# Low parts, decayed queries and masks in pieces of at most 512 columns, and a tie rule for activations, in a hybrid decoder step

## The chip, the cores and the metric

The kernel runs on one core of a Trainium2 chip. The metric is the device time of one execution in microseconds (us); the time given for a kernel is the median of several runs. Beside the runs there is one profiled execution, from which the trace comes. Its span runs from the first to the last instruction.

The engines are named as in the profile: PE is TensorE (matmuls; PEld its weight loads), DVE is VectorE, ACT is ScalarE, POOL is GpSimd, SP is SyncE, which issues most DMAs.

## The reference

One layer of a decoder for 1024 prompt tokens and 8 samples of 8 tokens each, 1088 columns in all, with a model width of 1024. Two branches work on the same input: sparse attention, in which a small indexer scores all keys and 256 are kept for each query, and gated linear attention (GLA). Both are projected, merged by gates, normalised, and followed by an MLP of width 4096. Cut to what matters here:

```python
def indexer_scores(q_idx, w_idx, k_idx):
    dots = jnp.einsum('bqhd,bsd->bqhs', q_idx, k_idx).astype(jnp.float32) * (IDX_DIM ** -0.5)
    w = w_idx.astype(jnp.float32) * (IDX_HEADS ** -0.5)
    return jnp.einsum('bqhs,bqh->bqs', jax.nn.relu(dots), w)
...
    def step(s, inp):
        qx, kx, vx, ax = inp
        cum = jnp.cumsum(ax, axis=-2)
...
        q_t = qx * jnp.exp(cum)
        k_t = kx * jnp.exp(-cum)
        att = jnp.where(causal, jnp.einsum('bhcd,bhed->bhce', q_t, k_t), 0.0)
        o = jnp.einsum('bhce,bhev->bhcv', att, vx) + jnp.einsum('bhcd,bhdv->bhcv', q_t, s)
...
def residual_block(x, mix_out, ln1_g, ln1_b, w_ff1, w_ff2, ln2_g, ln2_b):
    h = layer_norm(DN_ALPHA * x + mix_out, ln1_g, ln1_b)
    ff = jnp.square(jax.nn.relu(h @ w_ff1)) @ w_ff2
    return layer_norm(DN_ALPHA * h + ff, ln2_g, ln2_b)
```

The samples attend to 4096 cached keys each, which are read from a paged cache by a page table, for the indexer (64 wide) and for the attention (2 heads of 64).

## The kernel before

**Two parts of every number.** Matmuls of full precision are made of three faster ones. Each fp32 operand is split in a high part, which is a copy in the type fp32r, and a low part, which is the operand less its high part. A product is then high x high + high x low + low x high; the helper `mm3` issues the three. The high part is made by ScalarE (`act.activation(..., AF.Copy)`), the low part by a subtraction on VectorE or GpSimd, which the helper `sub` decides. Names in the profile follow this: `xh`, `xl`; `wh`, `wl`; `kih` and `kir` (the index keys' high part, and the raw page, which its low part overwrites); `ckh` and `ckl` (cached keys); `a` (both parts of an activation in one tile).

**An order chosen at build time.** The program is written by many generators (streams), for instance `idx_sample`, `gla_pre`, `at_scores` and `main`. Each yields what it needs next. The class `Order` asks every stream when its needs would be met and lets the first that is ready issue its next piece; the times come from `Clock`, which holds a modelled time for each engine and adds a modelled cost for every instruction. `Clock` also models that VectorE and GpSimd hold each other up on most of their operations. The engine queues then run in the order written, each waiting for the data of its instructions. `sub` reads the same modelled times: it takes GpSimd where that engine's time, plus 0.0021 us for each column, comes out before VectorE's, plus 0.00104 for each. So an edit of one instruction moves what is written after it, also on other engines and in streams that it doesn't touch. All instructions go through the helper at L266, so every row of the profile has that line, and work is told apart by the names of its tiles. The tokens stand in columns, in three chunks of 384, 384 and 320 (`CH`).

**The places that the change touches.**

- `idx_sample` (L880): the index keys of the samples come in 16 pages of 128x1024. `split(n)` copies page n to `kih` on ScalarE and subtracts into `kir`. Then `chunk` issues three matmuls `pss` for each 512 columns of the page: `kih`, `kir`, `kih`.
- `masks` (L1106): the masks of the prompt's query tiles, `msk`, are scaled by BIG on GpSimd, one instruction for each query tile, up to 1024 columns wide.
- `gla_pre` (L1291), once for each of four heads: the queries `gq` are multiplied by the decay `ge` on GpSimd, all 1088 columns, then the keys `gk` by its inverse `cu` on VectorE. `gla` (L1331) starts with `psas`, which needs the sample's 64 columns (the last) of both, and pads the sample's queries into `gqz`, 128x512, on GpSimd.
- `k_split` (L2404): the cached keys of the samples come in 32 pages of 128x1024 (two halves of 512 columns, one for each of two samples); ScalarE makes `ckh`, `sub` makes `ckl`, and `psc` matmuls use both. Their scores are summed into `as`, and VectorE adds the mask `msk` and takes the maximum in one custom instruction.
- `ff1_out` (L2670): after the eight matmul triples of a hidden block (`pf1`, in the profile `pf<-h,w`) ScalarE makes `fr`, the positive part, VectorE multiplies it by the matmul's result again to square it, ScalarE copies the high part into `a`, and `sub` makes the low part. The MLP works in groups: for the chunks 0 and 1, eight groups of four hidden blocks, in which the last activation is `a31` (block 3, chunk 1). The second matmuls (`pf2`, in the profile `pf<-a,w`) of a group follow its `pf1`, and meet `a31` as the last of the group's activations.

The stretches, in time: projections, indexer and GLA to about 885 us of the profile; output projections and the start of the MLP to 1155; the MLP of chunks 0 and 1 with the samples' attention beside it to about 1700; the samples' own output projections and the MLP of chunk 2 to the end.

Of the kernel before, what the change touches and what calls it, by code (L numbers as in the profile page):

```python
# [18 lines left out]
OP = mybir.AluOpType  # L19
# [4 lines left out]
P = 128  # L24
TP = 1024
TS = 64
T = TP + TS
# [8 lines left out]
CH = ((0, 384), (384, 384), (768, 320))  # L36
BIG = float(2.0 ** 100)
# [19 lines left out]
IAHEAD = 3  # L57
IFROM = 7
LATE_I = 1.5
FREER = 0.3  # L60
VAHEAD = 1
SCRATCH = 4096
# [30 lines left out]
def f32(ap):  # L93
    return ap.bitcast(F32)
# [292 lines left out]
def front(ph, tc, env, A, O):  # L387
    nc = tc.nc
    clock = env["clock"]
    pe, dve, act, pool, sp = env["eng"]  # L390
# [52 lines left out]
    def sub(out, a, b, late=0.0):  # L443

        n = out.free_size() if callable(out.free_size) else out.free_size
        if clock.t["pool"] + 0.0021 * n < clock.t["dve"] + 0.00104 * n + late:
            pool.tensor_tensor(out, a, b, op=OP.subtract)
        else:
            dve.tensor_sub(out, a, b)
# [179 lines left out]
    for c, (c0, n) in enumerate(CH):  # L629
        for k in range(KT):  # L630
            if c == 0 and k in (0, 4):
                h, l, r = (x[:, k:k + 4] for x in wtop)
                act.activation(h, r, AF.Copy)
                dve.tensor_sub(l, r, f32(h))
            s = slice(c0, c0 + n)
            r = xr[k - k % 2, c][:, k % 2, :n]
            act.activation(xh[k][:, s], r, AF.Copy)
            dve.tensor_sub(xl[k][:, s], r, f32(xh[k][:, s]))
        if c == 0:
            h, l, r = wnext  # L640
# [43 lines left out]
    bcol = csg("bcol", [P, 8, 64], BF)  # L684
# [146 lines left out]
    qz = page("qz", F32R, [P, 4, 2, P])  # L831
# [48 lines left out]
    def idx_sample():  # L880
        dve.memset(ss[1][0:64, TP:T], NEG)

        def split(n):
            r = raw[n]
            h = page(f"kih{n}", F32R, [P, 1024])
            act.activation(h, f32(r), AF.Copy)
            sub(r, f32(r), f32(h), LATE_I)
            raw[n] = (h, r)
        yield lambda: s_wtok.done
        cq = iota_f("cq", [4, 8, 8], [[0, 4], [0, 8], [1, 8]])  # L890
# [8 lines left out]
                                 selw, op0=OP.mult, op1=OP.mult)  # L899
# [206 lines left out]
    def masks(g, qts, gte):  # L1106
        if not mk:
            yield room("pg", 4)
        for i, grp in enumerate(MKP if not mk else ()):
            msk = page(f"msk{i}", BF, [P, 2 * T])  # L1110
            o = 0
            for qt in grp:
                mk[qt] = msk[:, o:o + (qt + 1) * P]
                o += (qt + 1) * P
        for j, qt in enumerate(qts):
            yield from fin(scp[qt], g.u[:, j:j + 1].bitcast(F32), mk[qt], gte)
            pool.tensor_scalar(mk[qt], mk[qt], BIG, None, op0=OP.mult)

    def top_first():
        yield lambda: s_ip.done  # L1120
# [170 lines left out]
    def gla_pre(h):  # L1291
# [32 lines left out]
        yield [cu]  # L1324
        act.activation(e, cu, AF.Exp, scale=1.0 / 16)
        act.activation(cu, cu, AF.Exp, scale=-1.0 / 16)
        pool.tensor_tensor(g["q"], g["q"], e, op=OP.mult)
        yield [cu]
        dve.tensor_tensor(g["k"], g["k"], cu, op=OP.mult)

    def gla(h):  # L1331
# [17 lines left out]
        dve.tensor_sub(vl[:TS], vs[:TS], f32(vh[:TS]))  # L1349
        pool.memset(f32(vl[TS:]), 0.0)  # L1350
        qz = small("gqz", 512).rearrange("p (a b) -> p a b", b=TS)
        pool.tensor_tensor(qz, q[:, None, TP:T].to_broadcast([P, 8, TS]), bcol, op=OP.mult)
        st = {}

        def half(i):
# [684 lines left out]
def back(ph, tc, env, A, O):  # L2040
# [20 lines left out]
    def own(name, shape, dt=F32, bufs=1):  # L2061
        return clock.take(pgs.tile(shape, dt, name=name, tag=name, bufs=bufs), name, "own " + name, bufs)

    def sub(out, a, b):
        n = out.free_size() if callable(out.free_size) else out.free_size
        if clock.t["pool"] + 0.0021 * n < clock.t["dve"] + 0.00104 * n:
            pool.tensor_tensor(out, a, b, op=OP.subtract)
        else:
            dve.tensor_sub(out, a, b)
# [334 lines left out]
    def k_split(n):  # L2404
        r = kraw.pop(n)
        h = wide(f"ckh{n}")
        l = wide(f"ckl{n}")
        act.activation(h, r, AF.Copy)
        sub(*(x.rearrange("p a b -> p (a b)") for x in (l, r, f32(h))))
        return h, l  # L2410

    def v_load(n):
# [257 lines left out]
    def ff1_out(ps, f, c, a):  # L2670
        n = CH[c][1]
        r = small("fr")
        act.activation(r[:, :n], ps[:, :n], AF.Relu)
        dve.tensor_tensor(r[:, :n], r[:, :n], ps[:, :n], op=OP.mult)
        t = page(f"a{f}{c}")
        act.activation(t[:, 0, :n], r[:, :n], AF.Copy)
        sub(t[:, 1, :n], r[:, :n], f32(t[:, 0, :n]))
        a[f, c] = (t[:, 0, :n], t[:, 1, :n])

    def ff2_pair(ws, c, a, np_):  # L2680
# [196 lines left out]
```

## Time and profile before

| | before |
|---|---|
| median of 3 runs | 2000.62 us (2000.35 to 2002.07) |
| the profiled execution | 2002.63 us |
| its span | 2000.9 us, 34496 instructions |
| mean granted TensorE clock | 0.997 |
| index pages' low parts, 128x1024 | 8 on VectorE (median 1227 ns), 8 on GpSimd (2402 ns) |
| cache pages' low parts, 128x1024 | 22 on VectorE (mean 1328 ns), 10 on GpSimd (2452 ns) |
| activations' low parts, 128x384 | 28 on VectorE (mean 587 ns), 36 on GpSimd (1018 ns) |

How rows of the profile are read: in the timeline, a row is start, length, engine, line, operation, tiles written <- tiles read, shapes and the count of like instructions in a row; in square brackets stands the engine's idle time before it and what ended that. In the groups by form, behind the bar stand the busy time in all, the mean of one in ns, and idle time before them. A row of waits is engine, tile <- what it waited for, then us in all, times, and the longest. A busy share near 100% on PE says only that matmuls were under way, since a matmul's recorded length overlaps the next one's.

### The profile page before, as it was taken

What the parts mean: (1) busy time and instruction counts of PE and PEld (TensorE: products, weight loads), DVE (VectorE), ACT (ScalarE), POOL (GpSimd) and SP (SyncE); (2) the same over time, 40 slices, a digit from 0 to 9 for tenths busy, and PEclk for the clock granted to TensorE, in tenths of its full rate; (3) what the DMA queues carried; (4) which work ended last, traced back from release to release, by engine and by line L of the source; (5) the groups of instructions that cost most, each with busy time, mean ns of one, the idle gap of its engine ahead of it and who ended that gap; (6) DMA issues with size and microseconds to landing.
All of it is one profiled execution on the core that took longest, in us unless ns stands there. A gap on an engine that the chain in (4) does not pass through costs nothing.

```text
span 2000.9 us, 34496 instructions
## 1 busy us (share of the span) xinstructions
PE 1977.4 (99%) x12341; PEld 1914.6 (96%) x12341; DVE 1288.1 (64%) x2704; ACT 1132.7 (57%) x2235; POOL 781.1 (39%) x640
## 2 busy tenths in 40 slices
PE   9999999999999999999999999999999999999998
PEld 8888999999999999999999999999999999999997
DVE  8887988777646856651366567777674445676635
ACT  6688778798667376660125345555654333455543
POOL 5133232232411422132233335646565543454455
PEclk9999999999999999999999999999999999999998
DMA  9564302213132243274751245545452354145542
GB/s 323 197 199 145 129 22 75 91 33 121 33 129 80 74 135 101 76 225 148 253 198 53 61 122 147 156 149 173 123 165 83 92 168 138 49 152 165 183 148 90
DMA packets 185164, 260.31 MB, mean 130 GB/s; under 512 B 22160, under 2 KB 121488, under 8 KB 184992
## 3 DMA queue, kind: packets, MB, share of 16 engines
q1 hardware_dynamic: 177440, 232.67, 36.6%
q0 software_dynamic: 7552, 25.43, 4.2%
q8 instruction: 97, 1.59, 0.3%
q14 instruction: 75, 0.61, 0.1%
HBM read 208.52 MB, written 49.51 MB: 129 GB/s over the span
## 4 chain that ended last, share of the span: by engine, by line
PE 64%; DVE 3%; ACT 2%; issue 2%; POOL 1%; DMA 1%; SPq 0%; ACTq 0%; POOLq 0%; DVEq 0%
PE pf L266 32%; PE gate L266 8%; PE pwo L266 5%; PE pmb L266 5%; PE gb L266 2%; PE pma L266 2%; PE psq L266 2%; PE pov L266 2%; PE ppt L266 2%; PE pob L266 1%; PE psc L266 1%; DVE as L266 1%; PE pst L266 1%; POOL w L266 0%; SPq L266 0%
## 5 line engine op out<-in xcount | busy, mean ns | idle before, releaser
L266 PE MATMUL pf<-a,w 128*128 128x384 f32 (+1 forms) x2304 | 398.6, 329 | 3.3 <-POOL a L266 1.3
L266 PE MATMUL pf<-h,w 128*128 128x384 f32 (+1 forms) x2304 | 395.2, 329 | 0.0
L266 PEld LDWEIGHTS pf<-a,w 128*128 128x128 f32 x2304 | 379.4, 188 | 7.8 <-ACT a L266 2.2
L266 PEld LDWEIGHTS pf<-h,w 128*128 128x128 f32 x2304 | 380.3, 188 | 2.9
L266 POOL TENSOR_TENSOR wl<-wr,wh 128x512 fp32r<-128x512 f32 (+1 forms) x135 | 171.4, 1291 | 405.1 <-ACT wh L266 319.3
L266 POOL TENSOR_TENSOR w<-wr,w 128x512 fp32r<-128x512 f32 x135 | 191.9, 1430 | 127.4 <-ACT w L266 118.4
L266 ACT ACTIVATE w<-wr 128x512 fp32r<-128x512 f32 x256 | 147.7, 619 | 34.1 <-PE pf L266 18.2
L266 DVE TENSOR_TENSOR w<-wr,w 128x512 fp32r<-128x512 f32 x121 | 124.4, 1033 | 51.8 <-ACT w L266 50.4
L266 DVE TENSOR_TENSOR acc<-acc,pf 128x384 f32<-128x384 f32 (+1 forms) x152 | 81.3, 538 | 82.1 <-PE pf L266 81.5
L266 PE MATMUL gate<-xh,wh 128*128 128x384 f32 (+1 forms) x384 | 130.1, 339 | 0.0
L266 PE MATMUL gate<-xh,wl 128*128 128x384 f32 (+1 forms) x384 | 125.6, 327 | 0.0
L266 PE MATMUL gate<-xl,wh 128*128 128x384 f32 (+1 forms) x384 | 125.6, 327 | 0.0
L266 POOL TENSOR_TENSOR a<-fr,a 128x384 fp32r<-128x384 f32 (+1 forms) x52 | 50.7, 976 | 181.4 <-ACT a L266 175.6
L266 ACT ACTIVATE wh<-wr 128x1024 fp32r<-128x1024 f32 (+1 forms) x76 | 75.2, 995 | 78.7 <-PE pmb L266 55.4
L266 ACT ACTIVATE a<-fr 128x384 fp32r<-128x384 f32 (+1 forms) x96 | 48.7, 507 | 105.8 <-DVE fr L266 105.8
L266 DVE TENSOR_TENSOR fr<-fr,pf 128x384 f32<-128x384 f32 (+1 forms) x96 | 50.7, 529 | 74.8 <-ACT fr L266 74.0
L266 ACT ACTIVATE jkb<-sc,gb_f 128x896 int8<-128x896 f32 (+2 forms) x96 | 86.1, 897 | 15.5 <-DVE gb_f L266 14.2
L266 ACT ACTIVATE fr<-pf 128x384 f32<-128x384 f32 (+1 forms) x96 | 44.6, 465 | 81.0 <-PE pf L266 79.9
L266 DVE TENSOR_SCALAR_CACHE_REDUCE jk<-sc,ga_f 128x1024 int8<-128x1024 f32 (+2 forms) x96 | 88.4, 921 | 2.2
L266 DVE CUSTOM_DVE_ANT_0 pp<-psq,msk 128x512 f32<-128x512 f32 (+3 forms) x96 | 51.2, 553 | 52.0 <-PE psq L266 45.4
L266 PE MATMUL psv<-wh,xh 128*128 128x256 f32 x288 | 80.8, 285 | 0.0
L266 PE MATMUL psv<-wl,xh 128*128 128x256 f32 x288 | 80.3, 283 | 0.0
(532 smaller groups left out, 5123.5 us busy)
## 6 DMA issues: line engine op xcount, KB each, us to landing
wr<-wff SPq DMA_DIRECT2D x254, 256.0 KB
wr<-w SPq DMA_DIRECT2D x42, 512.0 KB
ckr<-kT SPq DMA_DIRECT2D x256, 64.0 KB
ga_s<-gate SPq DMA_DIRECT2D x16, 544.0 KB
ci_s<-cig SPq DMA_DIRECT2D x16, 512.0 KB
kir<-ci_s SPq DMA_DIRECT2D x16, 512.0 KB
mgp<-ga_s SPq DMA_DIRECT2D x16, 384.0 KB
qa_s<-qa SPq DMA_DIRECT2D x8, 544.0 KB
```

Of the source, the lines that this page charges most:

```text
L266: r = f(*a, **k)
```

## The change

Five edits, in one diff:

- the index pages' low parts are made in two subtractions of 512 columns, each of which chooses its engine for itself;
- the scaling of the masks is cut at every 512 columns;
- the decay of the queries is cut in three, along the chunks 384, 384 and 320, and the padding of the sample's queries in two of 256;
- the cache pages' low parts are made in two subtractions of 512 columns, each choosing its engine;
- the activations' low parts go to GpSimd only if it comes out at least 0.5 us ahead by the modelled times (`A_LOW`); before, any lead was enough.

```diff
+A_LOW = 0.5
...
             act.activation(h, f32(r), AF.Copy)
-            sub(r, f32(r), f32(h), LATE_I)
+            for s in (slice(0, 512), slice(512, 1024)):
+                sub(r[:, s], f32(r[:, s]), f32(h[:, s]), LATE_I)
...
-            pool.tensor_scalar(mk[qt], mk[qt], BIG, None, op0=OP.mult)
+            for k0 in range(0, (qt + 1) * P, 512):
+                m = mk[qt][:, k0:min(k0 + 512, (qt + 1) * P)]
+                pool.tensor_scalar(m, m, BIG, None, op0=OP.mult)
...
-        pool.tensor_tensor(g["q"], g["q"], e, op=OP.mult)
+        for c0, n in CH:
+            s = slice(c0, c0 + n)
+            pool.tensor_tensor(g["q"][:, s], g["q"][:, s], e[:, s], op=OP.mult)
...
-        pool.tensor_tensor(qz, q[:, None, TP:T].to_broadcast([P, 8, TS]), bcol, op=OP.mult)
+        for s in (slice(0, 4), slice(4, 8)):
+            pool.tensor_tensor(qz[:, s], q[:, None, TP:T].to_broadcast([P, 4, TS]), bcol[:, s], op=OP.mult)
...
-    def sub(out, a, b):
+    def sub(out, a, b, sooner=0.0):
...
-        if clock.t["pool"] + 0.0021 * n < clock.t["dve"] + 0.00104 * n:
+        if clock.t["pool"] + 0.0021 * n + sooner < clock.t["dve"] + 0.00104 * n:
...
-        sub(*(x.rearrange("p a b -> p (a b)") for x in (l, r, f32(h))))
+        for i in range(2):
+            m = l.shape[1] // 2
+            sub(*(x[:, i * m:(i + 1) * m].rearrange("p a b -> p (a b)") for x in (l, r, f32(h))))
...
-        sub(t[:, 1, :n], r[:, :n], f32(t[:, 0, :n]))
+        sub(t[:, 1, :n], r[:, :n], f32(t[:, 0, :n]), A_LOW)
```

The edits move instructions on every engine from 119 us of the profile on. The three places below are the ones that the prediction speaks of. The added line shifts the helper from L266 to L267, and the numbers in the names count tiles, so a tile's number differs between the kernels.

The first is TensorE where the first index page is used, around 119 to 122 us (`ka` and `va` are matmuls of the projections, `pss` those of the index scores). Before:

```order
L266 MATMUL ka_2_1526<-xh7_125,wl5_0_1067 128x320
L266 MATMUL pss_1570<-kih0_1512,qz_314 128x512
L266 MATMUL pss_1570<-kir00_1506,qz_314 128x512
L266 MATMUL pss_1570<-kih0_1512,qz_314 128x512
L266 MATMUL pss_1576<-kih0_1512,qz_314 128x512
L266 MATMUL pss_1576<-kir00_1506,qz_314 128x512
L266 MATMUL pss_1576<-kih0_1512,qz_314 128x512
L266 MATMUL va_0_1610<-xh0_118,wh6_0_1290 128x384
```

And after, from the eighth of twelve `va` matmuls that now stand behind the same `ka`:

```order
L267 MATMUL va_0_1595<-xl2_128,wh6_0_1290 128x384
L267 MATMUL va_0_1595<-xh2_120,wl6_0_1291 128x384
L267 MATMUL va_0_1595<-xh3_121,wh6_0_1290 128x384
L267 MATMUL va_0_1595<-xl3_129,wh6_0_1290 128x384
L267 MATMUL va_0_1595<-xh3_121,wl6_0_1291 128x384
L267 MATMUL pss_1608<-kih0_1512,qz_314 128x512
L267 MATMUL pss_1608<-kir00_1506,qz_314 128x512
L267 MATMUL pss_1608<-kih0_1512,qz_314 128x512
L267 MATMUL pss_1614<-kih0_1512,qz_314 128x512
L267 MATMUL pss_1614<-kir00_1506,qz_314 128x512
L267 MATMUL pss_1614<-kih0_1512,qz_314 128x512
L267 MATMUL va_0_1595<-xh4_122,wh6_0_1290 128x384
```

So the six `pss` have moved behind twelve `va`. On GpSimd at the same place, before (`sc` are the prompt's index scores, whose diagonal is masked, `wl` the low part of a weight):

```order
L266 AFFINE_SELECT sc7_557<-sc7_557 128x128
L266 TENSOR_TENSOR kir01_1508<-kir01_1508,kih1_1567 128x1024
L266 TENSOR_TENSOR wl7_0_1607<-wr7_0_1288,wh7_0_1606 128x512 x2
L266 TENSOR_TENSOR kir10_1582<-kir10_1582,kih4_1676 128x1024
L266 TENSOR_TENSOR kir11_1641<-kir11_1641,kih5_1764 128x1024
```

and after:

```order
L267 AFFINE_SELECT sc7_557<-sc7_557 128x128
L267 TENSOR_TENSOR kir00_1506<-kir00_1506,kih0_1512 128x512
L267 TENSOR_TENSOR kir01_1508<-kir01_1508,kih1_1568 128x512 x2
L267 TENSOR_TENSOR kir02_1510<-kir02_1510,kih2_1622 128x512
L267 TENSOR_TENSOR wl7_0_1592<-wr7_0_1288,wh7_0_1591 128x512 x2
```

One half of the first page, `kir00`, is on GpSimd now, behind the select; it was whole on VectorE.

The second place is GpSimd at the third group of four hidden blocks, around 1268 to 1281 us (`cv` are cached values, `w` MLP weights, `a30` and `a31` the group's last two activations). Before:

```order
L266 TENSOR_TENSOR cv31_14303<-cvr3_14171,cv31_14303 128x512
L266 DMA cvr4_14306<-vv,ix_v_302 128x512 x2
L266 TENSOR_TENSOR ckl12_14360<-ckr12_14084,ckh12_14359 128x1024
L266 TENSOR_TENSOR w29_0_14399<-wr29_0_13982,w29_0_14399 128x512
L266 TENSOR_TENSOR cv41_14442<-cvr4_14306,cv41_14442 128x512
```

and after:

```order
L267 TENSOR_TENSOR cv31_14302<-cvr3_14149,cv31_14302 128x512
L267 DMA cvr4_14305<-vv,ix_v_302 128x512 x2
L267 TENSOR_TENSOR ckl12_14371<-ckr12_14081,ckh12_14370 128x512
L267 TENSOR_TENSOR a30_14408<-fr_14405,a30_14408 128x384
L267 TENSOR_TENSOR ckl13_14450<-ckr13_14181,ckh13_14449 128x512
L267 TENSOR_TENSOR a31_14484<-fr_14481,a31_14484 128x384
L267 TENSOR_TENSOR cv41_14500<-cvr4_14305,cv41_14500 128x512
```

Page 12 has one half on GpSimd, and the group's last two activations, which were on VectorE, stand on GpSimd, with a half of page 13 between them.

The third place is ScalarE at the eighth group, around 1721 to 1727 us (`h` and `z` belong to the LayerNorm of chunk 2, `lr` is its root, `lq` are squares for its sum). Before:

```order
L266 ACTIVATE lr_19356<-plv_19352,eps_101 128x3
L266 ACTIVATE fr_19370<-pf1_19339 128x384
L266 ACTIVATE a30_19373<-fr_19370 128x384
L266 ACTIVATE h02_19395<-z02_18789,lnp_100 128x320
L266 ACTIVATE h12_19398<-z02_18789,lnp_100 128x320
L266 ACTIVATE h22_19402<-z22_18791,lnp_100 128x320
L266 ACTIVATE h32_19412<-z22_18791,lnp_100 128x320
L266 ACTIVATE h42_19422<-z42_18931,lnp_100 128x320
L266 ACTIVATE fr_19424<-pf1_19376 128x384
L266 ACTIVATE a31_19427<-fr_19424 128x384
```

and after:

```order
L267 ACTIVATE fr_19414<-pf1_19389 128x384
L267 ACTIVATE a30_19417<-fr_19414 128x384
L267 ACTIVATE lq_19435<-z42_19079 128x320
L267 ACTIVATE lq_19439<-z62_19155 128x320
L267 ACTIVATE lq_19449<-z62_19155 128x320
L267 ACTIVATE fr_19458<-pf1_19420 128x384
L267 ACTIVATE a31_19461<-fr_19458 128x384
L267 ACTIVATE w89_0_19464<-wr89_0_18944 128x512
L267 ACTIVATE w90_0_19500<-wr90_0_19169 128x512
L267 ACT_TABLE_LOAD
L267 ACTIVATE lr_19516<-plv_19512,eps_101 128x3
L267 ACTIVATE h02_19545<-z02_18914,lnp_100 128x320
```

Five LayerNorm rows stood between `a30` and the last activation's `fr`; three squares stand there now, and the LayerNorm comes after `a31`.

## The prediction

> **What bounds the kernel.** I read the busy times first, then the chain that ended last.
>
> ```profile
> PE 1977.4 (99%) x12341; PEld 1914.6 (96%) x12341; DVE 1288.1 (64%) x2704; ACT 1132.7 (57%) x2235; POOL 781.1 (39%) x640
> PE 64%; DVE 3%; ACT 2%; issue 2%; POOL 1%; DMA 1%; SPq 0%; ACTq 0%; POOLq 0%; DVEq 0%
> ```
>
> TensorE (PE) is busy for 1977.4 of 2000.9 us, and the change neither adds nor removes a matmul. VectorE (DVE) and GpSimd (POOL) have hundreds of microseconds free, so an instruction there costs only when PE waits for its result. The question is which PE waits go and which arise.
>
> The written-out PE order is the same in both kernels up to 119 us of the profile, from 885 to 1155, and from about 1880 to the end. I take those stretches over at their old time. The two stretches where it moves, and three short ones that I need below:
>
> ```profile
> 70.40:72.20 1.80, 0.21 (x2) 0.00 (x0) 1.71 (x6) 0.69 (x3) 0.00 (x0) 1.00 0.85 344
> 72.30:75.60 3.30, 3.18 (x9) 3.03 (x10) 3.30 (x7) 1.96 (x4) 0.00 (x0) 0.50 0.97 313
> 75.70:79.10 3.40, 3.40 (x24) 3.34 (x23) 3.34 (x6) 1.46 (x3) 0.00 (x0) 1.00 0.14 57
> 119.00:885.00 766.00, 761.36 (x5004) 724.04 (x5004) 542.68 (x1430) 566.48 (x1169) 214.82 (x172) 1.00 0.33 102
> 1155.00:1880.00 725.00, 721.67 (x4381) 707.24 (x4380) 460.08 (x769) 356.47 (x662) 369.55 (x289) 1.00 0.45 137
> ```
>
> The columns are the window, its length, the busy time and count of PE, PEld, DVE, ACT and POOL, the granted clock, the DMA share and GB/s. PE is idle for 766.00 - 761.36 = 4.6 us and 725.00 - 721.67 = 3.3 us: 8 us in all are within reach. A row counts idle only from a matmul's modelled end, 0.33 us after its start, while matmuls of 128x384 start every 0.176 us (21 take 3.87 us below: 3.54 / 20). So a wait loses about 0.15 us more than its row says: some 10 us for the dozen or so waits. What they wait for, in the first stretch and then in the second:
>
> ```profile
> PE ppr L266 <- ACT jka L266: 1.9, 4, 0.6
> PE pss L266 <- DVE kir L266: 1.4, 1, 1.4
> ...
> PE psas L266 <- DVE gk L266: 0.3, 1, 0.3
> ```
> ```profile
> PE pf L266 <- ACT a L266: 0.7, 1, 0.7
> ...
> PE pf L266 <- POOL a L266: 0.6, 1, 0.6
> ```
>
> The change touches four of these: key pages `kir`, decayed keys `gk` (behind the queries on the shared pair of engines), and two waits for activations `a`.
>
> **Index key pages.**
>
> ```profile
> 118.96 0.40 PE L266 MATMUL pss<-kih,qz 128*128 128x512 f32 x1
> 119.44 1.21 DVE L266 TENSOR_TENSOR kir<-kir,kih 128x1024 fp32r<-128x1024 f32 x1
> 119.58 1.22 POOL L266 TENSOR_SCALAR_AFFINE_SELECT sc<-sc 128x128 f32<-128x128 f32 x1 [0.61 <-DVE sc L266]
> 120.71 0.50 PE L266 MATMUL pss<-kir,qz 128*128 128x512 f32 x1 [1.35 <-DVE kir L266]
> ```
>
> The first page's low part ends at 119.44 + 1.21 = 120.65, and PE starts the second `pss` at 120.71. It would have been due one spacing after 118.96, at 119.2, so 1.5 us are lost. Now the two halves are ordered apart: the first goes to VectorE and the second to POOL, and twelve `va` matmuls stand ahead of the six `pss` (12 x 0.176 = 2.1 us of work). PE reaches the second `pss` at 118.96 + 2.1 + 0.23 = 121.3; the first half ends near 119.44 + 0.7 = 120.1. The fifth, which needs the second half, is due some 0.7 later, at 122.0. That half stands on POOL behind the affine select (119.58 + 1.22 = 120.80) and takes about 1.3, to 122.1, so 0.1 to 0.2 is left. **Gain 1.3**. Bounds: 1.5 if the half is early, and nothing if POOL's select comes as much later as PE.
>
> What halves cost: the rows have whole pages on POOL, and a subtraction of the half's size, 128x512, of other data.
>
> ```profile
> L266 POOL TENSOR_TENSOR wl<-wr,wh 128x512 fp32r<-128x512 f32 x120 | 158.4, 1342 | 371.0 <-ACT wh L266 299.2 <-issue 29.2 <-PE pmb L266 18.6
> L266 POOL TENSOR_TENSOR kir<-kir,kih 128x1024 fp32r<-128x1024 f32 x8 | 19.2, 2400 | 25.6 <-ACT kih L266 25.6
> L266 POOL TENSOR_TENSOR ckl<-ckr,ckh 128x1024 fp32r<-128x1024 f32 x10 | 24.5, 2452 | 29.7 <-DMA ckr<-kT 18.3 <-ACT ckh L266 11.3
> ```
>
> Two halves on POOL are 2 x 1.342 = 2.68 against 2.40, 0.3 us more; on VectorE 2 x 0.69 (a row of the same size below) against 1.21, 0.2 more. Over 16 index pages and 32 cache pages that is some 10 us of engine time. It costs PE nothing, as the engines stand idle far longer than that before these very groups (25.6 us before `kir` on POOL). The same holds for the masks (eight scalings become sixteen) and the queries' pieces below: 15 us of POOL's 1220 idle ones. If the cover failed at one place, it would cost that half's 0.3.
>
> **Decayed queries.**
>
> ```profile
> 260.80 1.12 ACT L266 ACTIVATE cu<-cu 128x1088 f32<-128x1088 f32 x1
> 260.90 2.54 POOL L266 TENSOR_TENSOR gq<-gq,ge 128x1088 f32<-128x1088 f32 x1 [15.62 <-issue]
> 262.51 2.08 DVE L266 TENSOR_TENSOR gk<-gk,cu 128x1088 f32<-128x1088 f32 x1
> ```
> ```profile
> L266 DVE TENSOR_TENSOR gk<-gk,cu x4: 1275/1283/2078, 262.5 to 529.0; 128x1088 f32<-128x1088 f32 x4
> ```
>
> `gk` takes 2.08 where the other three heads have about 1.28: it starts while POOL's 2.54 us multiplication runs and gets through only when that ends at 263.44 (+ 1.15 = 264.59). PE's `psas` comes at 264.7, after a wait of 0.3 by its row, some 0.4 from start to start. With three pieces (384, 384, 320) VectorE gets in after the first or second. But the last piece, the sample's, then waits for `gk`, and `psas` needs both: that ends at about 260.90 + 2.54 + 1.28 + what three starts add (0.3), 265.0, later than now. What saves the term is that PE has six more matmuls ahead of `psas` and the `psa` ones earlier. I take **0.4**, from 0.4 (the wait goes) to -0.5 (`q` becomes the late one, 265.0 against 264.7 and the next heads alike). The three other heads have over a microsecond to spare. The `gqz` halves are of the same kind and shorter, and cost nothing.
>
> **Cache pages' low parts, third group of activations.**
>
> ```profile
> 1272.05 3.87 PE L266 MATMUL pf<-a,w 128*128 128x384 f32 x21
> ...
> 1272.51 2.40 POOL L266 TENSOR_TENSOR ckl<-ckr,ckh 128x1024 fp32r<-128x1024 f32 x1 [0.69 <-ACT ckh L266]
> 1272.83 2.63 DVE L266 CUSTOM_DVE_ANT_0 as<-as,msk 128x512 f32<-128x512 f32 x1
> ...
> 1275.49 0.55 DVE L266 TENSOR_TENSOR fr<-fr,pf 128x384 f32<-128x384 f32 x1
> ...
> 1276.66 1.21 PE L266 MATMUL pf<-a,w 128*128 128x384 f32 x3 [0.74 <-ACT a L266]
> ```
> ```profile
> 1304.12 0.69 DVE L266 CUSTOM_DVE_ANT_0 as<-as,msk 128x512 f32<-128x512 f32 x1
> ```
>
> VectorE's masking of `as` takes 0.69 when POOL is quiet, and 2.63 here: it ends 0.55 after POOL's page has ended (1274.91). Behind it on VectorE stands `fr`, the activation's square, then ScalarE's copy, the low part, and PE, whose cover of 21 matmuls has run out. PE loses 0.74 + 0.15 = 0.9, and 0.4 more one matmul later, where the low part ends: **1.3**. With a half page POOL's block is 1.34 long, so VectorE is free 1.1 us earlier even in the worst case; in the changed order, moreover, only one half of the page is on POOL, and four `psc` and four `pst` matmuls stand in the cover. The term lies between 1.3 and 0 (see the third rival).
>
> [...]
>
> **The tie.** The activation's low part goes to POOL only if POOL is free by half a microsecond more.
>
> ```profile
> L266 POOL TENSOR_TENSOR a<-fr,a 128x384 fp32r<-128x384 f32 x36 | 36.6, 1018 | 140.4 <-ACT a L266 134.6 <-DMA ckr<-kT 3.0 <-DMA wr<-wff 1.6
> L266 DVE TENSOR_TENSOR a<-fr,a 128x384 fp32r<-128x384 f32 x28 | 16.4, 587 | 16.5 <-ACT a L266 16.5
> ```
>
> One that moves is ready 1.018 - 0.587 = 0.43 earlier; by the order only three of 64 move. Only the last activation of a group (`a31`) is late for PE. By the order it goes VectorE, POOL, VectorE x5, POOL in the eight groups of before, and VectorE, VectorE, POOL, POOL, VectorE x3, POOL after. So the second group gains cover, and the third and fourth lose it. The eighth, before:
>
> ```profile
> 1721.94 4.03 PE L266 MATMUL pf<-a,w 128*128 128x384 f32 x22
> ...
> 1723.39 0.56 ACT L266 ACTIVATE h<-z,lnp 128x320 fp32r<-128x320 f32 x1 [0.36 <-DVE z L266]
> 1723.86 0.47 ACT L266 ACTIVATE fr<-pf 128x384 f32<-128x384 f32 x1
> ...
> 1725.56 1.00 POOL L266 TENSOR_TENSOR a<-fr,a 128x384 fp32r<-128x384 f32 x1 [5.54 <-ACT a L266]
> 1726.61 0.61 PE L266 MATMUL pf<-a,w 128*128 128x384 f32 x2 [0.64 <-POOL a L266]
> ```
>
> `fr` stands on ScalarE behind five LayerNorm rows `h` and starts 1.9 us after PE went on to `pf<-a`; PE loses 0.64 + 0.15 = 0.8. In the changed order the `h` rows come only after `a31`. POOL still has the subtraction, with a sum of the output norm ahead of it. I take **0.7**, between 0.8 and 0.
>
> What the third and fourth group may lose: from the start of `fr` to the end of `a31` on POOL are 1723.86 to 1726.56, 2.7 us, and with 0.4 from the matmul to `fr` 3.1. The cover is 21 matmuls, four `psc` and four `pst` in the third (about 4.9), 21 and four `pst` in the fourth (4.1). In both, `a31` stands on POOL directly behind a 128x512 subtraction of 1.3: 3.1 + 1.3 = 4.4 at the worst, a wait of 0 and 0.3; with ScalarE's queue as long as in the eighth group (1.5) 1.0 and 1.8. I take 0.7 for both together, nearest to the case without a queue. To it I add 0.5, a wait of the usual size in the rows above, for some place in the 1500 us that are dealt anew.
>
> **The sum**: 1.3 + 0.4 + 1.3 + 0.7 = 3.7 off, 0.7 + 0.5 = 1.2 back: 2.5 us less. The profiled execution spans 2000.9 and took 2002.63 with what lies around it; the span becomes 1998.4. That execution is above the median of the runs, 2000.62, so I take the same 2.5 from the median: **1998.1 us**.
>
> **Rivals.** *Waits only move.* The order is chosen anew from every changed duration, so other waits of the same size replace the named ones; PE's 99% speaks for it: within 1 us of 2000.6.
>
> *Much more goes.* If shorter blocks let VectorE and ScalarE run ahead at most places, most of the 10 us that the two stretches lose would go, say 6 to 7: 1994. Against it: half of that loss hangs on `ppr <- ACT jka` and others that no edit touches.
>
> *The cut frees nothing.* VectorE may not get in between two POOL instructions that stand back to back.
>
> ```profile
> 1492.34 2.53 POOL L266 TENSOR_TENSOR w<-wr,w 128x512 fp32r<-128x512 f32 x2
> ...
> 1493.13 3.54 DVE L266 CUSTOM_DVE_ANT_0 as<-as,msk 128x512 f32<-128x512 f32 x1
> ...
> 1494.83 1.28 POOL L266 TENSOR_TENSOR cv<-cvr,cv 128x512 fp32r<-128x512 f32 x1
> ...
> 1498.09 0.69 DVE L266 TENSOR_TENSOR cv<-cvr,cv 128x512 fp32r<-128x512 f32 x1
> ```
>
> Here the masking waited through three POOL instructions of 128x512 in a row. Elsewhere VectorE mostly gets in at the boundary. If this were the rule, the `ckl` term of 1.3 and the `gk` term of 0.4 would fall away: 2000.6 - 0.8 = 1999.8.
>
> *Slower: the clock halves at a group's boundary.* After PE's wait of about 1.8 us at 70.4 to 72.2, the window behind it has a granted clock of 0.50 for 3.3 us: nine matmuls, where the next window has 24 in 3.4. That costs some 1.7 us beyond the wait. The 1.4 us wait at 120.7 lies in a stretch of clock 1.00. So at the third and fourth group the price jumps where the wait for `a31` reaches about 1.8, that is where ScalarE's queue and POOL's half page both fall ahead of it: 1.8 + 1.7 = 3.5 at each. One of them gives -2.4 + 3.5, or 2001.7; both give -2.4 + 7.0, 2005.2. [...]
>
> **How the numbers follow.** 0.2% of 2000.62 is 4.0 us, about what a measurement of this kernel can tell from no change: faster is below 1996.6, slower above 2004.6. The forecast has 0.40 (0.04 of it below 1996.6), waits that only move 0.20, much more 0.27 (all below), the cut that frees nothing 0.04, the halved clock at both boundaries 0.09. Faster: 0.27 + 0.04 = 0.31; slower 0.09; same 0.60. The range runs from 1993.0, the large gain with a microsecond on top, to 2004.0, one halved clock with all the gains' lower ends; outside lie most of the slower case and the tail of the large gain, under 0.2.
>
> **What would show it.** In the changed trace: `pss <- kir` under 0.3; `gk` at 1.3 or an idle row that names `gq`; no masking row over 2 us ahead of the third group's `fr`; `pf <- a` waits at the third, fourth and eighth group under 0.4 each; PE's idle time in the two stretches about 5.5 instead of 8. A granted clock below 1 after 119 us, or a wait over 1 us for `a` on POOL, would make the forecast wrong upwards; `ppr <- ACT jka` gone, downwards.

## The result: slower, and the profile after

| | before | changed |
|---|---|---|
| median | 2000.93 us (4 runs) | 2012.43 us (2011.41 to 2012.99, 4 runs) |
| ratio | | 1.0053, 95% interval 1.0041 to 1.0065 |
| profiled execution, its span | 2002.63, 2000.9 us | 2011.41, 2009.7 us |

The change costs 11.5 us; 1998.1 was predicted, and the range ended at 2004.0. The page of the changed kernel, its span and busy times:

```profile
span 2009.7 us, 34589 instructions
PE 1979.5 (98%) x12341; PEld 1912.2 (95%) x12341; DVE 1288.2 (64%) x2721; ACT 1133.9 (56%) x2243; POOL 805.6 (40%) x679
```

POOL has 24.5 us more to do, and it is still idle for 60% of the time. PE has the same matmuls, so the loss is waiting. To find where, I compared the start of each matmul with that of its namesake before. In the profiled executions the lag goes from -1.8 us at 119 us to +2.6 at 895 us (4.4 lost), jumps by 2.4 at 1085 us, where the order is the same in both kernels, and grows by 4.1 more up to 1880 us. (The 1.8 us ahead at the start is a clock matter, at the end.) The two moved stretches, in the columns of the windows before (the first one's last wait now lies at 892 us, so it is taken a little longer):

```profile
119.00:895.00 776.00, 768.55 (x5039) 730.06 (x5038) 540.95 (x1434) 570.89 (x1178) 227.90 (x193) 1.00 0.33 102
1155.00:1890.00 735.00, 729.37 (x4415) 712.78 (x4414) 467.20 (x790) 357.09 (x665) 381.77 (x306) 1.00 0.45 136
```

PE is idle for 7.5 and 5.6 us there, where it was 4.6 and 3.3. (The lag grows by more than that, since a wait loses more than the idle time of its row.) The granted clock is 1.00, so the slower rival, a halved clock, is not what happened in this execution. The waits of PE in the first of them:

```profile
PE pov L267 <- DVE phl L267: 2.1, 2, 1.1
PE ppr L267 <- ACT jka L267: 1.1, 3, 0.6
PE ppt L267 <- ACT pp L267: 1.1, 1, 1.1
PE po L267 <- DVE Sm L267: 1.0, 1, 1.0
PE ppr L267 <- DVE gv L267: 0.9, 1, 0.9
...
PE pss L267 <- POOL kir L267: 0.2, 1, 0.2
```

and the longest in the second:

```profile
PE pf L267 <- POOL w L267: 1.2, 2, 0.7
PE pf L267 <- DVE w L267: 1.0, 2, 0.7
PE pf L267 <- DVE ptl L267: 0.8, 1, 0.8
PE pf L267 <- POOL a L267: 0.6, 1, 0.6
```

`kir` has shrunk from 1.4 to 0.2 and `gk` has gone, as forecast. Five waits of about 1 us stand in their place, for tiles that no edit touches: `pp` and `phl` (the prompt's attention weights), `Sm` and `gv` (GLA). In the second stretch the weights' low parts `w` come late. One of these places, with VectorE's and then POOL's, ScalarE's and PE's rows in the timeline of the changed kernel:

```profile
717.31 2.37 DVE L267 SCALAR_TENSOR_TENSOR eqs<-ssb,cgs,eqs 128x1088 int8<-128x1088 f32 x1
...
719.94 0.41 DVE L267 TENSOR_TENSOR phl<-ppt,phl 128x256 fp32r<-128x256 f32 x1
...
721.05 2.42 DVE L267 SCALAR_TENSOR_TENSOR eqs<-eqs,gts 128x1024 int8<-128x1024 int8 x2
723.39 0.15 DVE L267 RECIPROCAL rc<-mx 128x1 f32<-128x1 f32 x1
```
```profile
716.26 2.27 POOL L267 TENSOR_TENSOR wl<-wr,wh 128x512 fp32r<-128x512 f32 x1
```
```profile
723.64 0.72 ACT L267 ACTIVATE pp<-pp,rc 128x512 f32<-128x512 f32 x1 [4.15 <-DVE rc L267]
```
```profile
720.40 0.38 PE L267 MATMUL pov<-phl,vpr 128*128 128x256 f32 x1 [0.98 <-DVE phl L267]
...
724.41 0.98 PE L267 MATMUL ppt<-idf,pp 128*128 128x128 f32 x7 [1.06 <-ACT pp L267]
```

VectorE's queue holds work on the samples' key selection (`eqs`) ahead of `phl` and of `rc`, for which ScalarE's `pp` and then PE wait. The `eqs` of 1088 columns takes 2.37 beside POOL's `wl`, where the same instruction took 1.34 before, with POOL idle. Nothing here was cut: it is the order of the queues.

**The jump at 1085 us.** ScalarE writes the first row `h` of the first LayerNorm. The row before, and the last output-projection matmul of that kernel; then both, and PE's next matmul, of the changed kernel:

```profile
1079.95 1.14 ACT L266 ACTIVATE h<-zx,lnp 128x384 fp32r<-128x384 f32 x2 [4.52 <-DVE zx L266]
```
```profile
1082.20 0.34 PE L266 MATMUL pwo<-mh,wl 128*128 128x384 f32 x1
```
```profile
1085.17 1.12 ACT L267 ACTIVATE h<-zx,lnp 128x384 fp32r<-128x384 f32 x2 [7.19 <-PE pwo L267]
```
```profile
1084.79 0.34 PE L267 MATMUL pwo<-mh,wl 128*128 128x384 f32 x1
1085.83 0.44 PE L267 MATMUL pf<-h,w 128*128 128x384 f32 x1 [0.70 <-ACT h L267]
```

Before, `h` waited only for its input `zx` and came 2 us ahead of the last `pwo`. Now it starts when the last `pwo` has ended (1085.13), though it reads nothing of it. The built programs say why. The second half of the program lays its buffers over those of the first, and the first `h` row gets the buffer at address 44672 in both. Its last holder is another:

```
before   h00 at 44672, last held by wr70 (a raw weight, read last by VectorE)
changed  h00 at 44672, last held by wl70 (its low part, read by the last matmuls of pwo)
```

So the order of the instructions can be the same and the time not: the tiles were dealt to other buffers. In the built programs the first `h` row waits for VectorE before, and for PE in the changed kernel.

### The profile page after: what moved, and what is told of

The parts are those of the page before. It is cut to its first block, busy times and chain, and to the rows that moved or that the text cites. A ratio compares the mean times of both kernels' runs of the same rounds, so it can differ in the third digit from the quotient of the medians.

```text
span 2009.7 us, 34589 instructions
## 1 busy us (share of the span) xinstructions
PE 1979.5 (98%) x12341; PEld 1912.2 (95%) x12341; DVE 1288.2 (64%) x2721; ACT 1133.9 (56%) x2243; POOL 805.6 (40%) x679
## 4 chain that ended last, share of the span: by engine, by line
PE 77%; DVE 6%; issue 6%; ACT 4%; POOL 3%; DMA 2%; SPq 1%; ACTq 0%; POOLq 0%; DVEq 0%
PE pf L267 29%; PE gate L267 8%; PE psv L267 5%; PE pwo L267 5%; PE pmb L267 5%; PE gb L267 4%; PE qa L267 2%; PE pma L267 2%; PE kb L267 2%; PE qb L267 2%; PE psq L267 2%; PE pov L267 1%; PE ppt L267 1%; PE po L267 1%; PE pss L267 1%
## 5 line engine op out<-in xcount | busy, mean ns | idle before, releaser
L267 PE MATMUL pf<-a,w 128*128 128x384 f32 (+1 forms) x2304 | 399.2, 329 | 5.1 <-POOL a L267 1.3
L267 PE MATMUL pf<-h,w 128*128 128x384 f32 (+1 forms) x2304 | 396.5, 329 | 1.6 <-POOL w L267 0.7
L267 PEld LDWEIGHTS pf<-a,w 128*128 128x128 f32 x2304 | 379.0, 188 | 10.6 <-DVE w L267 1.9
L267 PEld LDWEIGHTS pf<-h,w 128*128 128x128 f32 x2304 | 379.8, 188 | 5.9 <-POOL w L267 1.1
L267 POOL TENSOR_TENSOR wl<-wr,wh 128x512 fp32r<-128x512 f32 (+1 forms) x135 | 174.5, 1314 | 381.7 <-ACT wh L267 292.4
L267 POOL TENSOR_TENSOR w<-wr,w 128x512 fp32r<-128x512 f32 x138 | 193.6, 1412 | 120.3 <-ACT w L267 108.4
L267 DVE TENSOR_TENSOR w<-wr,w 128x512 fp32r<-128x512 f32 x118 | 126.9, 1078 | 56.6 <-ACT w L267 53.7
L267 ACT ACTIVATE w<-wr 128x512 fp32r<-128x512 f32 x256 | 147.0, 618 | 20.3 <-DMA wr<-wff 9.9
L267 PE MATMUL gate<-xh,wh 128*128 128x384 f32 (+1 forms) x384 | 129.7, 338 | 0.0
L267 DVE TENSOR_TENSOR acc<-acc,pf 128x384 f32<-128x384 f32 (+1 forms) x152 | 80.5, 537 | 74.7 <-PE pf L267 74.1
L267 PE MATMUL gate<-xh,wl 128*128 128x384 f32 (+1 forms) x384 | 125.5, 327 | 0.0
L267 PE MATMUL gate<-xl,wh 128*128 128x384 f32 (+1 forms) x384 | 125.4, 327 | 0.0
L267 ACT ACTIVATE wh<-wr 128x1024 fp32r<-128x1024 f32 (+1 forms) x76 | 75.1, 995 | 78.4 <-PE pmb L267 58.0
L267 POOL TENSOR_TENSOR a<-fr,a 128x384 fp32r<-128x384 f32 (+1 forms) x49 | 47.6, 972 | 151.6 <-ACT a L267 149.4
L267 ACT ACTIVATE a<-fr 128x384 fp32r<-128x384 f32 (+1 forms) x96 | 48.7, 507 | 102.6 <-DVE fr L267 102.6
L267 DVE TENSOR_TENSOR fr<-fr,pf 128x384 f32<-128x384 f32 (+1 forms) x96 | 50.7, 529 | 73.1 <-ACT fr L267 72.3
L267 ACT ACTIVATE jkb<-sc,gb_f 128x896 int8<-128x896 f32 (+2 forms) x96 | 86.2, 898 | 11.7 <-DVE gb_f L267 9.3
L267 ACT ACTIVATE fr<-pf 128x384 f32<-128x384 f32 (+1 forms) x96 | 44.7, 466 | 82.8 <-PE pf L267 82.7
L267 DVE TENSOR_SCALAR_CACHE_REDUCE jk<-sc,ga_f 128x1024 int8<-128x1024 f32 (+2 forms) x96 | 88.3, 920 | 2.0
L267 PE MATMUL psv<-wh,xh 128*128 128x256 f32 x288 | 80.7, 284 | 0.0
L267 PE MATMUL psv<-wl,xh 128*128 128x256 f32 x288 | 80.3, 283 | 0.0
L267 DVE CUSTOM_DVE_ANT_0 pp<-psq,msk 128x512 f32<-128x512 f32 (+3 forms) x96 | 51.4, 553 | 44.0 <-PE psq L267 43.7
```

Source lines behind the costliest of these rows:

```text
L267: r = f(*a, **k)
```

## The experiments

Two theories at first. A: what costs is the new deal, of order, of buffers and of the engines that `sub` and its like choose, which any change of an instruction's modelled time sets off. B: the pieces themselves cost. The front's edits and the back's act on separate stretches, so they were taken apart first. The kernel before was run again beside each group of experiments, and "more" and "less" are against its median there: 2001.44, 2001.02 or 2001.44 us.

**Index pages, masks and queries alone.** The diff is the changed kernel's, without `k_split` and `A_LOW`.

> The index pages', masks' and queries' edits alone; cache pages and activations as before. By its written order the first 885 us are those of the changed kernel and the rest those of the kernel before. Theory A (the loss comes from what is dealt anew: the order of the instructions, and the buffers that tiles get): between 119 and 885 us the changed trace lost 4.4 us against the one before, and 2.4 us more at 1085 us, where ScalarE's first h row waits for the last output-projection matmul; so 6.8 us more than before, about 2007.7, with that wait at h present. Theory B (the pieces themselves cost: 32 more instructions here, 32 in the cache pages): half of the 11.5 us, about 2006.6. Rival to the wait at h: it belongs to the later stretch, and this kernel is at 2005.3.

Measured: 2008.01 us, 6.6 more than the 2001.44 of before in that job; ratio 1.0032 (1.0020 to 1.0045).

**Cache pages and activations alone.** The rest of the diff.

> The cache pages' and activations' edits alone. By its written order all up to 1155 us is the kernel before. Theory A: the later stretch lost 4.1 us against the one before, so about 2005.0, and no PE wait at h around 1085 us. Theory B: half of 11.5, about 2006.6.

Measured: 2005.65, 4.2 more; 1.0017 (1.0007 to 1.0026). The two losses, 6.6 and 4.2, add up to 10.8, near the 11.5, and each has about the size that theory A gave it; theory B's equal halves, 5.75 each, lie outside the second's interval (1.4 to 5.2).

**All cuts, but the old order.** The clock is told of one whole instruction, and the two halves are issued past it. For the cache pages:

```diff
-        sub(*(x.rearrange("p a b -> p (a b)") for x in (l, r, f32(h))))
+        e = pool if on_pool else dve
+        for i in range(2):
+            y = [z[:, i * 512:(i + 1) * 512] for z in x]
+            e.raw.tensor_tensor(*y, op=OP.subtract) if on_pool else e.raw.tensor_sub(*y)
+        clock.note(e.name, "tensor_tensor" if on_pool else "tensor_sub", tuple(x), ...)
```

> The four cuts are made, but the modelled clock is told of one whole instruction each time, so that every other instruction, every engine choice and every buffer stay as in the kernel before; both halves of a page stay on one engine, and the tie rule is left as before. Theory A: nothing is dealt anew, only the named gains that don't hang on a new order are left (first index page half as long, 0.6; shorter holds): 1999 to 2001. Theory B: the pieces cost whatever the order, 2008 to 2012.

Measured: 2000.54, 0.9 less; 0.9996 (0.9986 to 1.0006). Theory B falls as the reason of the 11.5 us: with all four cuts made and the order kept, nothing is lost in all. The masking in the third group, VectorE's and POOL's rows of this run:

```profile
1271.16 1.52 DVE L266 CUSTOM_DVE_ANT_0 as<-as,msk 128x512 f32<-128x512 f32 x1
```
```profile
1270.84 3.00 POOL L2430 TENSOR_TENSOR ckl<-ckr,ckh 128x512 fp32r<-128x512 f32 x2 [0.69 <-ACT ckh L266]
```

It ends at 1272.68, before POOL's second half does (1273.84): 1.52 instead of 2.63, as VectorE gets in between the halves. PE's 0.7 us wait for `a` there is gone, and the lag falls by 1.4 us. (The trace of before has such an entry too: at 230.15 us a VectorE instruction of 128x3, `gb_m`, with a median of 0.16 us, took 1.26 beside the first of four `wl` of POOL, which began at 230.08 and took 5.06 together. It ended at 231.41, 3.7 us before the last of the four.) From 1390 to 1500 us 2.5 us are lost again, at waits for `as` and `ptl`. So the cut of the cache pages is not free even in the old order: in this execution it gained 1.4 and lost 2.8 in all. The run further down with whole cache pages has no such loss.

**Another buffer for the first `h` row.** In the changed kernel, a later page takes the buffer first, by a memset of one column:

```diff
+            if f == c == 0:
+                acc[3, 0] = page("acc60", F32)
+                pool.raw.memset(acc[3, 0][:, 0, 0:1], 0.0)
             t = page(f"h{f}{c}") if c < 2 else xpage(f"h{f}{c}", F32R)
-            if f % 2 == 0 and c < 2:
+            if f % 2 == 0 and c < 2 and (f, c) != (6, 0):
```

> The changed kernel with one GpSimd memset of one column more, which takes over the first free page buffer ahead of the first h row, so that this row gets another buffer; the order is otherwise that of the changed kernel. Theory A: h no longer waits for the last output-projection matmul, 2.4 us less than the changed kernel, about 2010.0. Rival: the wait hides another one behind it (POOL's or VectorE's rows there), and the time stays within 0.8 us of 2012.4.

Measured: 2009.95, 2.5 less than the changed kernel's 2012.43 (8.5 more than before instead of 11.5). In the trace the lag is 4.2 on both sides of this place, where it jumped by 2.4. The wait now stands on POOL, which has nothing else to do, and ScalarE is free of it:

```profile
1086.76 0.10 POOL L2316 MEMSET acc<- 128x1 f32 x1 [2.07 <-PE pwo L267]
```
```profile
1084.10 1.14 ACT L267 ACTIVATE h<-zx,lnp 128x384 fp32r<-128x384 f32 x2 [4.55 <-DVE zx L267]
```

This one point is settled: 2.4 of the 11.5 us.

**The edits one by one.** First the index pages alone.

> The index pages' cut alone. Up to about 250 us the order is that of the changed kernel, so the gain at the first index page (1.1 in the changed trace) is here too. The buffer of the first h row was last read 25 matmuls before the output projection ends, 4.4 us earlier than in the changed kernel: no wait at h around 1085 us. If this cut is what deals the loss of 119 to 885 us: 2001.4 - 1.1 + 5.5 = 2005.8. If that loss belongs to the masks' and queries' cuts: 2000.3.

Measured: 2004.85, 3.8 more (1.0009 to 1.0028). No wait at `h`, as the buffer's last holder said. Its longest new wait is in GLA:

```profile
PE po L266 <- ACT Sm L266: 3.0, 2, 2.2
```

From 391.6 us on, 0.9 us after the longer of these two waits, the granted clock was 0.50 for 3.4 us.

Then masks and queries alone.

> The masks' and the queries' cuts alone. The buffer of the first h row was last read by the last matmul of the output projection: the 2.4 us wait at h is back, by that alone 2003.8. If these cuts also deal the loss of 119 to 885 us, 2003.8 + 5 = 2009; if not, 2003 to 2004.

Measured: 2002.44, 1.4 more (0.9996 to 1.0015), with the wait at `h` (0.7 for `h`, 0.7 for `plm`, 0.2). Less than forecast, so elsewhere it gained 1 us. The losses don't add up: 3.8 and 1.4 apart, 6.6 together. Each set of edits has a deal of its own.

**The same deal without the cuts.** Here no instruction is cut; the clock is told of the pieces:

```diff
+            for k0 in range(0, (qt + 1) * P, 512):
+                m = mk[qt][:, k0:min(k0 + 512, (qt + 1) * P)]
+                clock.note("pool", "tensor_scalar", (m, m, BIG, None), {"op0": OP.mult})
-            pool.tensor_scalar(mk[qt], mk[qt], BIG, None, op0=OP.mult)
+            pool.raw.tensor_scalar(mk[qt], mk[qt], BIG, None, op0=OP.mult)
```

and alike for the queries.

> No instruction is cut. Only the modelled clock is told of the pieces of masks and queries, so that order, engines and buffers are those of the run with these cuts alone, and the instructions are those of the kernel before. Theory A: within 1.5 us of that run, with the 2.4 us wait at h: about 2003.8 or more. Theory B: 2001.4, as before.

Measured: 2005.45, 4.4 more than before (1.0008 to 1.0027), though every instruction is that of before; some run on another engine (ScalarE has 2242 instead of 2235, POOL 635 instead of 640). It is 3.0 slower than the run with these cuts (2002.44), where the expectation allowed 1.5; each median is uncertain by about 2. So in this order the cuts may save something, how much is not shown: of the 3.4 us between the two profiled executions at the end, 1.9 were there at 118 us, ahead of any cut, by the clock matter at the end.

**The cache pages alone**, with the old tie rule:

> The cache pages' cut alone, the tie rule as before. By its order it is the run of both up to about 1450 us, where that one had lost 4.5 us against before and later won 0.7 at the eighth group. If the cut alone carries the loss: 2005 to 2006.5; if the tie rule does: about 2001.

Measured: 2008.68, 7.7 more (1.0021 to 1.0044), worse than expected. Up to 1450 us it lags like the run of both, then loses 3 us more; its longest wait for `ptl` is 2.6 us, at 1502, which the tie rule's deal avoids. So the tie rule is worth some 3 us here, by way of the deal.

**The cuts of the front in the old order**, cache pages whole:

> As the pinned run, but the cache pages whole: index pages, masks and queries cut, order, engines and buffers as before. The pinned run's trace gained 1.0 us by 340 us and gave it back only after 1390, at waits behind cache pages. So 2000.0 to 2000.3, no loss later. Rival: the cut's gain is within the spread of the runs and the time is 2001.

Measured: 2000.20, 1.2 less (0.9987 to 1.0006): the expected size, within what can be told from none.

**One engine for both halves.** Theory C: the halves on two engines hold each other. POOL's halves of index pages in the changed kernel, and in the run with the old order, where both are on one engine:

```profile
L267 POOL TENSOR_TENSOR kir<-kir,kih 128x512 fp32r<-128x512 f32 x18 | 29.2, 1626 | 35.2 <-ACT kih L267 35.2
```
```profile
L447 POOL TENSOR_TENSOR kir<-kir,kih 128x512 fp32r<-128x512 f32 x16 | 20.3, 1292 | 25.6 <-ACT kih L266 25.5
```

A half takes longer there, 1.63 against 1.29 us, so they do seem to hold each other. Whether that costs time:

```diff
+        on_pool = clock.t["pool"] + 0.0021 * 1024 < clock.t["dve"] + 0.00104 * 1024
         for i in range(2):
+            pool.tensor_tensor(*y, op=OP.subtract) if on_pool else dve.tensor_sub(*y)
```

> The cache pages' cut alone, but one choice for both halves of a page, as for whole pages before (the run of the cut with a choice for each half: 2008.7). Theory A (dealing): the order is again another one from 1250 us on, and most of the 7.7 us comes from what it happens to put late; 2003 to 2008. Theory C: what costs is that the two halves of a page run on VectorE and GpSimd at once and hold each other (1.6 us for a half on GpSimd instead of 1.3); then 2001 to 2002.

Measured: 2010.41, 9.0 more (1.0027 to 1.0061), more even than the forecast of A. With both halves on one engine the loss is as large, so C is not its reason; what C alone costs was not measured apart. And the same deal with whole pages:

> No instruction is cut; the modelled clock alone is told of two halves on one engine. Order, engines and buffers are those of the run before this one. Theory A: within 1.5 us of that run, or slower than it by what shorter instructions save. Theory B (pieces cost): faster than it, 2001.

Measured: 2009.29, 7.9 more (1.0024 to 1.0049), with no instruction cut. At 1755 us this kernel is 1.3 us ahead of the one before, and from 1770 on 5.7 behind: the loss lies at one place. PE's waits between 1690 and 1850 us, VectorE's queue and a window there:

```profile
PE pf L266 <- DVE h L266: 3.1, 1, 3.1
PE plm L266 <- POOL ls L266: 1.9, 1, 1.9
```
```profile
1757.84 3.79 DVE L266 TENSOR_TENSOR w<-wr,w 128x512 fp32r<-128x512 f32 x3
1761.55 0.53 DVE L266 SCALAR_TENSOR_TENSOR z<-z,lnp,plr 128x320 f32<-128x320 f32 x1
1762.01 0.54 DVE L266 SCALAR_TENSOR_TENSOR h<-z,lnp,h 128x320 fp32r<-128x320 f32 x1
```
```profile
1760.00:1764.00 4.00, 1.40 (x5) 1.24 (x6) 4.00 (x7) 1.16 (x3) 1.08 (x1) 0.80 0.66 235
```

The LayerNorm of chunk 2 has come too late for its matmuls, and three weights' subtractions stand ahead of its row `h` on VectorE. After that wait of 3.1 us the granted clock is down as well, 0.80 in the window: it was 0.50 for 3.4 us from 1762.4 on. In the run with the cut pages it was 0.50 for 6.8 us at the same place, and for 3.4 us at 1499; that can be why it was the slower of the two by 1.1 us.

**One figure of the modelled clock.** No cut, one modelled cost 1% higher:

```diff
-            return 0.13 + n * 0.0009 if op in ("affine_select", "memset") else 0.175 + n * 0.0022
+            return 0.13 + n * 0.0009 if op in ("affine_select", "memset") else 0.175 + n * 0.00222
```

> The kernel before with one figure of the modelled clock changed by 1% (0.00222 instead of 0.0022 us for each column on GpSimd); no instruction is cut, added or left out, but the order is dealt anew from 450 us on. Theory A: it costs a few us like the others, 2003 to 2006. Rival: only the particular cuts deal badly, and this one is within 1 us of 2001.

Measured: 2005.52, 4.1 more (1.0011 to 1.0032). Its two longest waits behind the cache pages:

```profile
PE pf L266 <- DVE as L266: 2.5, 1, 2.5
PE psc L266 <- DVE ptl L266: 1.9, 1, 1.9
```

Behind the wait of 2.5 us the granted clock was 0.50 here too, for 3.4 us from 1500.6 on. Half of 3.4 is 1.7 us of matmul time, an estimate of what a deal can cost by the clock, beyond its waits. The mean clock of this kernel's eight runs is 0.995 to 0.997, that of the kernel before beside them 0.996 to 0.998.

That is theory A by itself. Three kernels in which not one instruction was cut, added or left out lost 4.1, 4.4 and 7.9 us by a new deal. In each of them some instructions also changed engine (in the last, VectorE has 2712 instead of 2704, ScalarE 2229 instead of 2235, POOL 638 instead of 640). What order, engines and buffers cost apart from each other is shown only for the buffer of `h`. The cuts under a given deal brought 0.9 and 1.2 us (old order), 3.0 (masks and queries), and -1.1 (cache pages on one engine), none of them far outside the spread of the runs.

## Why the prediction was wrong, step by step

**Right.** PE's waits as the measure, and the independence of the stretches (6.6 and 4.2 apart, 11.5 together). The index page: 1.3 forecast, and its wait went from 1.52 to 0.32 us, start to start. That is right in size and in part by luck, since the halves lie the other way round than the text has them. In the changed kernel POOL's rows, VectorE's and PE's are:

```profile
117.77 0.69 POOL L267 TENSOR_SCALAR_AFFINE_SELECT sc<-sc 128x128 f32<-128x128 f32 x1 [0.61 <-DVE sc L267]
118.43 3.85 POOL L267 TENSOR_TENSOR kir<-kir,kih 128x512 fp32r<-128x512 f32 x3
```
```profile
117.62 0.68 DVE L267 TENSOR_TENSOR kir<-kir,kih 128x512 fp32r<-128x512 f32 x1
```
```profile
119.77 0.50 PE L267 MATMUL pss<-kir,qz 128*128 128x512 f32 x1 [0.15 <-POOL kir L267]
```

The first half, for which the second `pss` waits, is POOL's and stands behind the select; the second half is VectorE's. With the text's own times for POOL (the half ends at 122.1, and PE comes at 121.3) 0.8 us would have been left of the wait, and the gain been 0.7. It was 1.2 because the select took 0.69 here instead of 1.22, which the text did not foresee. The decayed queries: 0.4 forecast, and the wait of 0.42 is gone; `gk` is at 1.28 us for all four heads:

```profile
L267 DVE TENSOR_TENSOR gk<-gk,cu x4: 1275/1278/1286, 257.0 to 532.2; 128x1088 f32<-128x1088 f32 x4
```

The eighth group: 0.7 forecast, 0.85 gone. That halves cost PE nothing on engines that stand idle holds for index pages, masks and queries in the old order; the cache pages' gave back more than they gained there, as said above.

**The third group: the masking came free earlier, and the place gave nothing.** Its masking, the way of `a31` through ScalarE and POOL, and PE's rows after the change:

```profile
1277.73 0.70 PE L267 MATMUL pf<-h,w 128*128 128x384 f32 x3
...
1278.09 1.43 DVE L267 CUSTOM_DVE_ANT_0 as<-as,msk 128x512 f32<-128x512 f32 x1
...
1278.93 1.21 ACT L267 ACTIVATE as<-psc 64x512 f32<-64x512 f32 x2 [1.04 <-PE psc L267]
...
1280.71 1.04 ACT L267 ACTIVATE ckh<-ckr 128x1024 fp32r<-128x1024 f32 x1
...
1281.66 0.47 ACT L267 ACTIVATE fr<-pf 128x384 f32<-128x384 f32 x1
...
1281.88 1.79 POOL L267 TENSOR_TENSOR ckl<-ckr,ckh 128x512 fp32r<-128x512 f32 x1 [2.91 <-ACT ckh L267]
...
1283.15 0.52 ACT L267 ACTIVATE a<-fr 128x384 fp32r<-128x384 f32 x1 [1.02 <-DVE fr L267]
...
1283.73 0.44 PE L267 MATMUL pf<-a,w 128*128 128x384 f32 x1 [0.27 <-ACT a L267]
1283.75 1.00 POOL L267 TENSOR_TENSOR a<-fr,a 128x384 fp32r<-128x384 f32 x1
...
1284.81 0.62 PE L267 MATMUL pf<-a,w 128*128 128x384 f32 x2 [0.64 <-POOL a L267]
```

The masking took 1.43 instead of 2.63, beside POOL's low part of `a30` (1.00 us) instead of a whole page. But `fr` stands on ScalarE behind `as`, `cv` and `ckh` and starts at 1281.66, 3.2 us after the last matmul that it reads has ended (1278.43). So `a31` has its high part only at 1283.67, and its low part, now on POOL, is 1.00 long. POOL's half page ahead of it ends at 1283.67 too, so it delays nothing. PE lost 0.43 and 0.91 us, as much as before. For this group the prediction had a wait of 0, or 1.0 "with ScalarE's queue as long as in the eighth group", and it took 0.7 for both groups, "nearest to the case without a queue"; the third, with the queue, had 1.34, the fourth none. So of the term of 1.3 and the 0.7 set against it, this place made nothing in all. That the whole 1.3 would come back, out of a range of 0 to 1.3, was the author's estimate, and no run of the changed order shows it; in the old order the lag fell by 1.4 us at this place.

**The step that failed first**: "To it I add 0.5, a wait of the usual size in the rows above, for some place in the 1500 us that are dealt anew." The first stretch lost 4.4 net of gains of 1.2 + 0.4, so 6.0 us of new waits; the second 4.1 net of 0.85, so 5.0. Against 0.5 stood 11, and PE's idle time in the two stretches rose from 8 us to 13.1, where the prediction had 5.5. The text treated a new deal as neutral: the old waits that no edit names would stay or be replaced by others of their size. The rival "waits only move" rested on the same idea. The runs showed that every other deal that ran took longer than the one before, by 1.4 us (which can't be told from none) to the 11.5 of the changed kernel, whatever set it off. Nothing in the profile of before shows that; a null edit beside it would have. Why the old deal is the better one stays open.

**The step that failed second**: "I take those stretches over at their old time." At 1085 us the order was the same and 2.4 us were lost, to a buffer whose last holder had changed. The order's waits would have shown it before any run: the first `h` row of the changed kernel has a wait for PE that it didn't have.

**The slower rival** had the right side and the wrong mechanism. The wait for `a31` was 0.9 us at the most, and the clock did not fall in either stretch of the changed kernel's profiled execution. In other deals it did, mostly behind waits of 2.2 to 3.1 us, as the experiments show.

The sum as measured: 2.45 of named gains, 11 of new waits, 2.4 at `h`: 10.9 us, beside 11.5 (8.2 to 13.0) between the medians. The 11 are what the lag leaves, not a count of single waits.

What stays open: which order would keep the cuts' gains and the old one's few waits. The cache pages' deal with whole pages was 1.3 us ahead at 1755 us; a version with its late LayerNorm mended was not tried.

## What to carry to other kernels

Where a planner with modelled times writes the order, an edit's price is that of its instructions plus that of a new deal, and the second can be ten times the first; a null edit, one modelled figure changed by 1%, gives its size. One such edit was run here, and the deals differ (1.4 to 11.5 us), so several would be better. To judge an edit by itself, issue it past the planner and keep the old order and buffers. An equal order is not an equal program: compare the waits too, above all where a later phase reuses an earlier one's buffers.

## What the hardware showed unasked

After a wait of PE at 70 us the clock falls in some executions only. The changed kernel's rows for that place and the stretch behind it:

```profile
69.90:71.80 1.90, 0.30 (x2) 0.00 (x0) 1.78 (x7) 0.78 (x3) 0.00 (x0) 1.00 0.75 304
71.90:75.20 3.30, 3.18 (x18) 3.03 (x19) 3.29 (x7) 2.24 (x5) 0.00 (x0) 1.00 1.00 312
```

There are 18 matmuls at a clock of 1.00, where before had nine at 0.50, with the same instructions ahead of them. Of the 14 profiled executions of this study seven have the halved stretch and seven have not, across kernels; with it PE comes out some 1.5 us later. Part of it goes by the length of the wait. In nine executions the matmul behind it starts 2.15 or 2.16 us after the one ahead of it, and seven of these have the halved stretch; in the other five it is 1.87 to 2.12 us, and none has it. Length alone does not decide, though: later on, 2.51 us (index pages alone) and 2.80 us (one modelled figure) were followed by a clock of 0.50, 2.84 us (cache pages alone) was not, and in the run with one choice for both halves 1.42 us was. The 1.5 us are part of why 8.8 us lie between the two profiled spans and 11.5 between the medians; whether they are part of the spread between the runs of one kernel was not shown, as each kernel was profiled in one execution.
